# 528-column tiles for the high weight parts of a streamed decoder layer: five buffers at five offsets

## The chip, the cores and the metric

One core of a Trainium2 chip runs the whole kernel in one launch. The metric is the device time in microseconds (us) of one execution. The kernel before was timed three times: 2457.62, 2460.19 and 2460.8 us, median 2460.19 us. Addresses below are bytes within one SBUF partition.

## The reference

One decoder layer on 256 tokens of width 2048, in fp32. Cut to what matters, with D = 2048:

```
h  = rms_norm(x) * (1 + scale1) + shift1
z  = h @ w_in + b_in                       # combined input projection
y_attn = nsa_attention(q, k..., v...) @ w_nsa_out
y_conv = conformer_conv(a_glu) @ conv_pw_w + conv_pw_b
x  = x + gate1 * ((g0 * y_attn + g1 * y_conv) @ w_out)
h2 = rms_norm(x) * (1 + scale2) + shift2
# PEER: 16384 experts, 8 heads, 16 experts for each head and token
a    = einsum('td,ted->te', h2, u_emb[experts])
coef = gelu(a) * gate
out  = x + gate2 * einsum('te,ted->td', coef, v_emb[experts])
```

The kernel computes the PEER part densely: all 16384 rows of `u` and `v` are read, and a token's coefficient is zero for the experts that it did not choose.

## The kernel before

Nearly all of the work is TensorE (PE) matmuls whose weights stream in from HBM once. The class `Stream` (lines 129 to 219) walks a plan of weight pieces. A piece is 128 partitions x 512 columns of fp32. For each, SyncE loads half of a `raw` tile (line 149), ScalarE (ACT) rounds it to the type float32r as the high part `hi` (lines 152 and 153), and VectorE (DVE) computes the low part `lo` = raw - hi (lines 157 to 159). `hi` has five buffers, `lo` four, `raw` four of two pieces each. Three pieces are prepared ahead of the one that PE works on. There are 774 planned loads, so 1548 pieces. The order of everything is written out by hand: each call of `piece` issues the matmuls of one piece and then advances the side jobs (convolution, attention, top-k, and so on).

A piece is used in one of three ways:

- `proj` (lines 200 to 202), 524 pieces: `hi` and `lo` are the stationary operand, 128 columns at a time, and 256 token columns are the moving operand. Each piece gives 12 matmuls: hi x high activations, hi x low activations, lo x high activations, four times. In 32 of these pieces (the first eight half-head projections of `peer_wq`) the moving operand is `uhi` or `ulo`, 258 columns wide, so its start moves on by 1032 bytes from each k to the next.
- `proj2` (lines 213 and 217), 512 pieces of `u`: four matmuls with `hi` stationary and 512 moving columns of `h2`, then four with `lo` stationary and 256 moving columns.
- `products` (lines 1313 to 1315), 512 pieces of `v`: here `hi` and `lo` are the moving operand, 512 columns, and the coefficients `chi` and `clo` are stationary. For each of two token halves: chi x hi, chi x lo, clo x hi. For the first 49 rows of `v` (196 pieces) `chi` and `clo` lie in the pool `gg`, where they take the buffers that are called ohA, ohB, Ahi and Alo in the trace; for the other 79 rows (316 pieces) they lie in the pool `vp`.

Float32r matmuls read 4 bytes of the moving operand for each column and partition. A weight load (LDWEIGHTS) of 128 columns is part of every matmul and runs while the matmul before it streams.

Memory is handed out from both ends of the partition. `const` and `stream` lie at the low end, and the pools opened later with no side (`xp`, `adap`, `qkv`, `cp`, `attn`, `x1p`, `mp`, `tk`, `cb`) follow above them. The pools with `side="right"` come down from the high end. Sizes added up in that order give these starts, modulo 512 bytes:

| tiles | start modulo 512 before |
|---|---|
| `hi`, all five buffers (2048 bytes each) | 32 |
| `lo`, all four buffers | 32 |
| `hhi`, `hlo`, `ohi`, `olo`, `yhi`, `ylo`, `h2`: moving operands in pools from the right | 480 |
| `mhi`, `mlo`: moving operands of `w_out`, in `mp` (a pad tile of 448 bytes lies below them) | 480 |
| `uhi` for k = 0, 1, 2, ... | 160, 168, 176, ... |
| `chi`, `clo` in `gg` (v rows 0 to 48) | 480 |
| `chi`, `clo` in `vp` (v rows 49 to 127) | 288 |

Each 128-column slice of `hi` or `lo` is 512 bytes, so all slices of a buffer start at the same value.

Of the kernel before, what the change touches and what calls it, by code (L numbers as in the profile page):

```python
# [10 lines left out]
F32R = mybir.dt.float32r  # L11
# [61 lines left out]
def build(nc, tc, d):  # L73
# [19 lines left out]
    stream = P("stream")  # L93
# [33 lines left out]
    AHEAD = 3  # L127

    class Stream:
# [11 lines left out]
        def prefetch(self, to):  # L141

            last = 2 * len(self.chunks) - 1
            while self.hi_done <= min(to + 1, last):
                n = self.hi_done
                while self.loaded <= min(n // 2 + 3, len(self.chunks) - 1):
                    raw = stream.tile([128, 1024], F32, name="raw", tag="raw", bufs=4)
                    src, shape = self.chunks[self.loaded]
                    sp.dma_start(raw.rearrange("p (a b) -> p a b", a=shape[0]), src)
                    self.raw[self.loaded] = raw  # L150
                    self.loaded += 1
                hi = self.his[n] = stream.tile([128, 512], F32R, name="hi", tag="hi", bufs=AHEAD + 2)
                sc.copy(hi, self.source(n))  # L153
                self.hi_done += 1
            while self.lo_done <= min(to, last):
                n = self.lo_done
                lo = stream.tile([128, 512], F32R, name="lo", tag="lo", bufs=AHEAD + 1)
                hi = self.his.pop(n)
                ve.tensor_sub(lo, self.source(n), hi.bitcast(F32))  # L159
                self.parts[n] = (hi, lo)  # L160
                if n % 2:
                    del self.raw[n // 2]
                self.lo_done += 1
# [1271 lines left out]
```

## Time and profile before

| what | value |
|---|---|
| times of three runs | 2457.62, 2460.19, 2460.8 us |
| time of the profiled execution | 2459.97 us |
| its span, first to last instruction | 2458.2 us |
| PE busy | 2423.1 us (99%), 15324 matmuls |
| DVE busy | 1941.6 us (79%) |
| ACT busy | 1427.6 us (58%) |
| POOL busy | 140.4 us (6%) |
| HBM read | 533.41 MB, 219 GB/s over the span |

The profiled execution lies 1.8 us above its own span and 0.2 us below the median of the three runs. A matmul's duration in the profile runs from its start to the modelled end of its results, and matmuls overlap; the time that a matmul costs is the distance to the start of the next one, called its pitch here. In a stretch where PE is busy throughout, the mean pitch is the stretch plus one duration, divided by the number of matmuls that the view counts in it.

### The profile page before, as it was taken

How to read it: one execution, taken by the hardware profiler on the slowest of the kernel's cores; microseconds unless marked ns; L12 is line 12 of the kernel's file. 1: busy time of each engine (PE TensorE's matmuls, PEld its weight loads, DVE VectorE, ACT ScalarE, POOL GpSimd, SP SyncE). 2: the span in 40 equal slices, each digit the busy share in tenths (PEclk: the TensorE clock that was granted, in tenths of full speed). 3: DMA queues.
4: the chain of work that ended last, by engine and by line, in shares of the span. 5: the costliest groups of instructions: out<-in, count | busy, mean ns of one | idle time of the engine just before them, and what ended most of it. 6: DMA issues, size and time to landing. Idle time of an engine off the chain costs nothing.

```text
span 2458.2 us, 44220 instructions
## 1 busy us (share of the span) xinstructions
PE 2423.1 (99%) x15324; PEld 2152.0 (88%) x15324; DVE 1941.6 (79%) x4136; ACT 1427.6 (58%) x3198; POOL 140.4 (6%) x262
## 2 busy tenths in 40 slices
PE   6999999999999999999999999999999999999999
PEld 5899999888899999988888888888888888888887
DVE  7989897889788877899988888888655566666665
ACT  1045456667455566555568888887555555555554
POOL 0000000211222210000000000000000000100100
PEclk9999999999999999999999999999999999999999
DMA  9965556755888985555555555555555567777765
GB/s 374 400 222 192 186 190 196 242 176 188 300 298 306 322 275 170 186 190 187 192 189 173 178 173 180 174 179 173 189 193 191 192 211 243 241 243 242 243 204 195
DMA packets 155170, 540.49 MB, mean 220 GB/s; under 512 B 18753, under 2 KB 19009, under 8 KB 154689
## 3 DMA queue, kind: packets, MB, share of 16 engines
q1 hardware_dynamic: 134178, 467.40, 55.7%
q0 software_dynamic: 20768, 70.27, 9.1%
q8 instruction: 120, 1.97, 0.3%
q14 instruction: 104, 0.85, 0.1%
HBM read 533.41 MB, written 4.19 MB: 219 GB/s over the span
## 4 chain that ended last, share of the span: by engine, by line
PE 84%; issue 7%; DVE 5%; DMA 2%; POOL 2%; SPq 0%; POOLq 0%; ACT 0%; DVEq 0%
PE ps_acc L213 19%; PE ps_acc L217 10%; PE acc L200 7%; PE acc L202 7%; PE acc L201 7%; DVE acc L309 3%; PE ps_o L1315 2%; PE ps_s L1315 2%; PE ps_t L1315 2%; PE ps_o L1314 2%; PE ps_s L1314 2%; PE ps_t L1314 2%; PE ps_acc L1315 2%; PE ps_acc L1314 2%; PE ps_o L1313 2%
## 5 line engine op out<-in xcount | busy, mean ns | idle before, releaser
L153 ACT CAST hi<-raw 128x512 fp32r<-128x512 f32 x1548 | 956.1, 621 | 808.3 <-PE acc L201 246.5
L159 DVE TENSOR_TENSOR lo<-raw,hi 128x512 fp32r<-128x512 f32 x1548 | 1062.7, 688 | 390.6 <-PE ps_o L1314 78.4
L213 PE MATMUL ps_acc<-h,hi 128*128 128x512 f32 x2048 | 564.6, 397 | 0.0
L213 PEld LDWEIGHTS ps_acc<-h,hi 128*128 128x128 f32 x2048 | 346.7, 188 | 44.2
L217 PEld LDWEIGHTS ps_acc<-h,lo 128*128 128x128 f32 x2048 | 311.4, 188 | 46.4
L200 PE MATMUL acc<-hhi,hi 128*128 128x256 f32 x1200 | 345.7, 288 | 0.0
L202 PE MATMUL acc<-hhi,lo 128*128 128x256 f32 x1200 | 332.8, 277 | 0.2 <-DVE lo L159 0.2
L201 PE MATMUL acc<-hlo,hi 128*128 128x256 f32 x1200 | 332.8, 277 | 0.0
L217 PE MATMUL ps_acc<-h,lo 128*128 128x256 f32 x2048 | 318.0, 277 | 0.0
L200 PEld LDWEIGHTS acc<-hhi,hi 128*128 128x128 f32 x1200 | 225.7, 188 | 6.3 <-issue 5.3
L201 PEld LDWEIGHTS acc<-hlo,hi 128*128 128x128 f32 x1200 | 226.1, 188 | 3.2 <-issue 3.1
L202 PEld LDWEIGHTS acc<-hhi,lo 128*128 128x128 f32 x1200 | 225.4, 188 | 0.4 <-DVE lo L159 0.4
L371 POOL DMA_DIRECT2D adaw<-in_w_ada_dram x192 | 104.7, 546 | 774.3 <-DVE rr L719 277.3
L385 DVE SCALAR_TENSOR_TENSOR ada<-adaw,sc_c,ada 128x512 f32<-128x512 f32 x180 | 134.4, 746 | 14.4 <-DMA adaw<-in_w_ada_dram 13.9
L1290 POOL DMA_DIRECT2D g2w<-in_w_ada_dram x64 | 34.4, 538 | 1404.3 <-DVE Alo L123 1098.5
L1205 ACT ACTIVATE Ahi<-ohA,high 128x128 f16<-128x128 f16 x256 | 100.7, 393 | 10.4 <-PE ps_o L1226 10.2
L471 DVE SCALAR_TENSOR_TENSOR cacc<-glu,dwh,cacc 128x256 f32<-128x256 f32 x240 | 105.1, 475 | 0.0
L341 PE MATMUL zb<-hr,w 128*128 128x256 f32 x448 | 99.8, 381 | 0.0
L1205 ACT ACTIVATE Alo<-ohA,low 128x128 f16<-128x128 f16 x256 | 99.1, 387 | 0.0
L341 PEld LDWEIGHTS zb<-hr,w 128*128 128x128 f32 x448 | 84.5, 191 | 11.0
L309 DVE SCALAR_TENSOR_TENSOR acc<-wa,sc_c,acc 128x256 f32<-128x256 f32 x224 | 91.3, 478 | 0.0
L200 PE MATMUL acc<-ohi,hi 128*128 128x256 f32 x256 | 72.1, 282 | 3.7 <-DVE mr L903 3.7
(371 smaller groups left out, 4528.0 us busy)
## 6 DMA issues: line engine op xcount, KB each, us to landing
raw<-in_u_dram SPq DMA_DIRECT2D x256, 512.0 KB, 3.6
raw<-in_v_dram SPq DMA_DIRECT2D x256, 512.0 KB, 4.4
raw<-in_w_in_dram SPq DMA_DIRECT2D x150, 512.0 KB, 4.2
adaw<-in_w_ada_dram POOLq DMA_DIRECT2D x192, 256.0 KB, 5.0
wa<-in_w_ada_dram SPq DMA_DIRECT2D x64, 512.0 KB, 9.0
raw<-in_nsa_out_dram SPq DMA_DIRECT2D x32, 512.0 KB, 5.8
raw<-in_w_out_dram SPq DMA_DIRECT2D x32, 512.0 KB, 5.7
raw<-in_peer_wq_dram SPq DMA_DIRECT2D x32, 512.0 KB, 3.7
```

The lines of the kernel that those rows point to most:

```text
L153: sc.copy(hi, self.source(n))
L159: ve.tensor_sub(lo, self.source(n), hi.bitcast(F32))
L200: pe.matmul(ps, hi[:, o:o + 128], xhi[:, k], start=(k == 0), stop=False)
L201: pe.matmul(ps, hi[:, o:o + 128], xlo[:, k], start=False, stop=False)
L202: pe.matmul(ps, lo[:, o:o + 128], xhi[:, k], start=False, stop=(k == nk - 1))
L213: pe.matmul(ps.rearrange("p a t -> p (a t)"), hi[:, o:o + 128], x[:, k].rearrange("p a t -> p (a t)"), start=(k == 0), stop=False)
L217: pe.matmul(ps[:, 1], lo[:, o:o + 128], x[:, k, 0], start=False, stop=(k == nk - 1))
L309: ve.scalar_tensor_tensor(a, raw[:, i], c, a, op0=OP.mult, op1=OP.add)
L341: pe.matmul(zb[n // 2][:, n % 2], ws[k][n // 7][:, n % 7], hr[k], start=(k == 0 and n % 2 == 0), stop=(k == KT - 1), skip_group_check=True)
L1205: sc.activation(part[:, j], A[:, j], AF.Copy, scale=g[:, t0 + j:t0 + j + 1])
L1314: pe.matmul(ps, chi, lo, start=False, stop=False)
L1315: pe.matmul(ps, clo, hi, start=False, stop=(i1 == NK - 1))
```

## The change

The `hi` tile is allocated 528 columns wide, and its first 512 columns are used.

```
@@ -149,7 +149,7 @@
                     sp.dma_start(raw.rearrange("p (a b) -> p a b", a=shape[0]), src)
                     self.raw[self.loaded] = raw
                     self.loaded += 1
-                hi = self.his[n] = stream.tile([128, 512], F32R, name="hi", tag="hi", bufs=AHEAD + 2)
+                hi = self.his[n] = stream.tile([128, 528], F32R, name="hi", tag="hi", bufs=AHEAD + 2)[:, 0:512]
                 sc.copy(hi, self.source(n))
                 self.hi_done += 1
```

A buffer is then 2112 bytes, 64 more than four times 512. The five buffers start at 32, 96, 160, 224 and 288 modulo 512. All that lies above them at the low end moves up by 320 bytes: `lo` to 352, `mhi` and `mlo` to 288. The pools from the right stay where they are. The narrowest place, between the low and the high stack, is around the tiles `C1` and `C0`: 448 bytes before, 128 after. No instruction, wait, DMA or shape is added or removed.

## Rows read from the trace of the kernel before

**Rows 1.** The page, parts 1 and 2: busy us (share); PE and its clock in 40 slices.
```profile
PE 2423.1 (99%) x15324; PEld 2152.0 (88%) x15324; DVE 1941.6 (79%) x4136; ACT 1427.6 (58%) x3198; POOL 140.4 (6%) x262
PE   6999999999999999999999999999999999999999
PEclk9999999999999999999999999999999999999999
```
**Rows 2.** Groups of instructions by line: count, busy us, mean ns, idle before by releaser.
```profile
L159 DVE TENSOR_TENSOR lo<-raw,hi 128x512 fp32r<-128x512 f32 x1548 | 1062.7, 688 | 390.6 <-PE ps_o L1314 78.4 <-ACT hi L153 76.3 <-PE acc L202 58.9
L153 ACT CAST hi<-raw 128x512 fp32r<-128x512 f32 x1548 | 956.1, 621 | 808.3 <-PE acc L201 246.5 <-PE ps_acc L213 148.2 <-PE ps_o L1315 91.6
```
**Rows 3.** PE stretches: from:to us, length, busy (matmuls), clock, DMA share, GB/s.
```profile
160.00:208.00 48.00, 48.00 (x426) 1.00 0.58 193
1060.00:1240.00 180.00, 180.00 (x1041) 1.00 0.57 190
1800.00:2000.00 200.00, 200.00 (x876) 1.00 0.59 191
2060.00:2380.00 320.00, 320.00 (x1413) 1.00 0.72 238
```
**Rows 4.** Line 200 by tile: duration ns min/median/max, first to last start us, form.
```profile
L200 PE MATMUL acc<-hhi,hi x1200: 276/276/684, 148.7 to 803.7; 128*128 128x256 f32 x172
L200 PE MATMUL acc<-ohi,hi x256: 276/276/552, 642.8 to 814.5; 128*128 128x256 f32 x128
L200 PE MATMUL acc<-mhi,hi x256: 276/276/367, 814.9 to 905.7; 128*128 128x256 f32 x128
L200 PE MATMUL acc<-yhi,hi x128: 276/281/684, 560.1 to 631.0; 128*128 128x256 f32 x128
L200 PE MATMUL acc<-h,hi x128: 276/278/366, 956.3 to 1003.9; 128*128 128x256 f32 x128
```
**Rows 5.** Timeline of PE in a `proj` of `peer_wq`: start us, duration us, matmul.
```profile
962.72 0.28 PE L200 MATMUL acc<-h,hi 128*128 128x256 f32 x1
...
964.49 0.28 PE L200 MATMUL acc<-h,hi 128*128 128x256 f32 x1
```
**Rows 6.** Timeline of PE in a `proj` with 258 moving columns of `uhi` and `ulo`.
```profile
931.76 0.29 PE L200 MATMUL ps_o<-uhi,hi 128*128 128x258 f32 x1
...
933.92 0.28 PE L200 MATMUL ps_o<-uhi,hi 128*128 128x258 f32 x1
```
**Rows 7.** Line 213, the 512-column matmuls of `u`: duration ns min/median/max.
```profile
L213 PE MATMUL ps_acc<-h,hi x2048: 388/398/483, 1004.3 to 1748.9; 128*128 128x512 f32 x187
```
**Rows 8.** Timeline of PE where `chi` moves from `gg` (ohA) to `vp`.
```profile
2017.84 0.39 PE L1315 MATMUL ps_acc<-hi,ohB 128*128 128x512 f32 x1
...
2018.53 0.39 PE L1315 MATMUL ps_acc<-hi,ohB 128*128 128x512 f32 x1
2018.76 0.40 PE L1313 MATMUL ps_o<-hi,chi 128*128 128x512 f32 x1
2018.99 0.39 PE L1314 MATMUL ps_o<-lo,chi 128*128 128x512 f32 x1
...
2020.14 0.39 PE L1313 MATMUL ps_s<-hi,chi 128*128 128x512 f32 x1
```
**Rows 9.** Lines 153 and 159 alone: duration ns min/median/max, first to last start us.
```profile
L153 ACT CAST hi<-raw x1548: 601/622/701, 138.6 to 2445.7; 128x512 fp32r<-128x512 f32 x194
L159 DVE TENSOR_TENSOR lo<-raw,hi x1548: 627/691/696, 139.5 to 2446.9; 128x512 fp32r<-128x512 f32 x194
```

More of the change, by code (lines that the diff above doesn't have):

```diff
@@ L151, in prefetch @@
                     self.loaded += 1
-                hi = self.his[n] = stream.tile([128, 512], F32R, name="hi", tag="hi", bufs=AHEAD + 2)
+                hi = self.his[n] = stream.tile([128, 528], F32R, name="hi", tag="hi", bufs=AHEAD + 2)[:, 0:512]
                 sc.copy(hi, self.source(n))
```

## The prediction

> **What bounds the kernel now.** I read the page first: PE is busy for 2423.1 of 2458.2 us, at nine tenths or more in all slices but the first, and its clock shows nine in every slice [rows 1]. So the time is the sum of PE's pitches, and what the other engines do matters only where PE waits. Next the preparation: ACT's rounding and DVE's subtraction take 956.1 and 1062.7 us in all and wait mostly for PE to give a buffer back [rows 2]; they follow PE. Their durations hardly spread (median 622 of 601 to 701 ns, and 691 of 627 to 696 ns [rows 9]), so I see nothing in them that depends on which buffer they touch.
>
> Then the pitch, in stretches where PE never pauses. The granted clock is 1.00 there, the level of 2.4 GHz [rows 3]. Let the length plus one matmul's duration be divided by the count:
>
> - `proj`, 256 columns, 160 to 208 us: 48.28/426 = 113.3 ns. At 2.4 GHz this is 272 cycles, 17 for every 16 columns.
> - `u`, 1060 to 1240 us: 180.39/1041 = 173.3 ns, or 1.386 us for the eight matmuls of a piece. At the rate above, four of 512 and four of 256 columns would take 1.360 us. So 0.026 us of each `u` piece is excess.
> - `v` with coefficients in `gg`, 1800 to 2000 us: 200.39/876 = 228.8 ns. By the rate above 512 columns take 226.7 ns. Excess 2.1 ns a matmul, 0.013 us a piece.
> - `v` with coefficients in `vp`, 2060 to 2380 us: 320.39/1413 = 226.7 ns. No excess.
>
> The last two run the same instructions on the same `hi` and `lo`; what differs is that the stationary operand starts at 480 modulo 512 in one and at 288 in the other. The step between them lies in the open [rows 8]: three matmuls before it take 2018.53 - 2017.84 = 0.69 us, the six after it 2020.14 - 2018.76 = 1.38 us against 1.36 us at the rate, the first alone 0.23 us, and then the excess is gone for good. No wait shows there. I take from it that PE's pitch depends on where the stationary and the moving operand lie relative to each other, and that a new relation is settled into at a price.
>
> Two more stretches show the same. In `proj` of `peer_wq`, where all offsets are as elsewhere, 15 matmuls take 964.49 - 962.72 = 1.77 us, 118.0 ns each [rows 5], so one relation has two states, at 113.3 and at 118 ns. The duration shows which: its median is 276 ns for `hhi`, `ohi` and `mhi`, 281 for `yhi`, 278 for `h2` [rows 4]; most of `proj` is in the quick state. And where the moving operand starts 8 bytes further on at every k and its high and low parts differ, 18 matmuls of 258 columns take 933.92 - 931.76 = 2.16 us, 120.0 ns each [rows 6], against 258/256 x 113.3 = 114.2 ns at the rate: 5.8 ns of excess, with no settling.
>
> **The change, part by part.** Nothing is added to any queue. ACT writes and DVE reads the same 512 columns; I cost that at nothing, since 1548 of each show no spread by buffer [rows 9] and both have idle time [rows 2]. The buffers succeed each other as before, everything low moves by the same 320 bytes, and the two stacks still do not meet, so no wait changes its partner.
>
> What moves is the relation between `hi` and its partner. So far it is the same in every piece of a stage. After the change it differs from one piece to the next, five in turn, and within a piece `hi` and `lo` (352) differ as well. So every piece boundary is such a step as the one of [rows 8]. I price a step at that row's 0.02 us (1.38 - 1.36) and put it on all pieces but the 32 with `uhi`, which have no fixed relation to lose:
>
> - `proj`, (1200 + 256 + 256 + 128 + 128)/4 = 492 pieces [rows 4]: 492 x 0.02 = +9.8 us.
> - `u`, 512 pieces: they pay 0.026 us each already; I let the step replace this and count 0.
> - `v` in `gg`, 196 pieces: 0.02 - 0.013 = 0.007 each, +1.4 us.
> - `v` in `vp`, 316 pieces: +6.3 us.
>
> Sum +17.5 us. Against it, PE waits for `hi` or `lo` here and there in `proj` (maxima of 684 and 552 ns against medians of 276 [rows 4]) and in `u` (483 against 398 [rows 7]); a later PE finds its buffers ready, and some of the slow `proj` state goes. I take off 3.5 us for both, a fifth, as an estimate. The forecast is 2459.97 + 14 = 2474 us, as close to the median, 0.2 us away.
>
> Bounds of the price, since no row shows `hi` and `lo` at differing offsets: upward the 5.8 ns a matmul of the stretch that never settles [rows 6]; downward that excess vanishes wherever the offsets are far apart, as it does in `vp` [rows 3], so below nothing. My value lies nearest to [rows 8], because each piece keeps one relation for six to twelve matmuls, and that row shows six as enough to settle.
>
> The row says that a matmul is slowed by 10 to 20 ns in all when only an operand's address changes [rows 8]. The Trainium skill, "SBUF — State Buffer", section "Who interferes with whom", states that PE has two independent read ports, one for the moving operand and one for weight loads, and that PE never waits on anyone. By that rule the change would be worth nothing, and the sum would be 2460 us; the trace here speaks against it, and I keep it as a rival only.
>
> **Rivals.**
>
> - Nothing moves (2460 us). The excess would belong to the phase in which PE starts a stage, not to the addresses, and the step of [rows 8] would be chance. For: one relation has two states [rows 4, 5]. Against: the step falls on the very matmul where the address changes.
> - Faster (2446 us). The excess belongs to operands that lie within 64 bytes of each other modulo 512: 480 against 32 in `proj`, `u` and `v` in `gg`; in `vp`, 288 against 32, there is none [rows 3]. After the change four of five `hi` buffers and `lo` are further away in `proj` and `u`. `u` would give back four fifths of 512 x 0.026 = 13.3 us, 10.7 us; `proj` some 4 us of its slow state; `v` in `gg` 2 us; `v` in `vp`, now mixed (288 against 32 to 288 and 352), would lose 316 x 0.013 x 0.6 = 2.5 us. Sum -14 us. It decides if a step between two distant relations costs under some 0.009 us, so that 1516 of them stay below 14 us. Against: the `uhi` stretch has its operands 128 bytes and more apart and is the slowest of all [rows 6].
> - Much slower (2513 us). No piece settles: 5.8 ns on each of 5904 `proj` matmuls (34 us) and 1896 in `vp` (11 us), 5.8 - 2.1 on 1176 in `gg` (4 us), 5.8 - 3.3 on 4096 in `u` (10 us), less the same absorbed part, some 6 us: +53 us. Against: every relation that lasts has settled so far.
>
> The change could also fail to do what it says if the allocator rounded the tile up to 2560 bytes; then nothing would move, and the first rival's time holds.
>
> **How the numbers follow.** Forecast (a price for each step, +5 to +35 us) 0.45; nothing 0.19; faster 0.25; much slower 0.11. Slower holds the first and the last, 0.56. Differences below 0.2% (4.9 us) can't be told from no change. The forecast's own range is 2465 to 2495 us. For 8 in 10, I leave out the lower half of the faster case and most of the much slower one: 2444 to 2500 us.
>
> **What the profile after would show.** Right: the stretch of `v` in `vp` rises from 226.7 to some 230 ns a matmul; `proj` durations of 281 ns and above become common where 276 ruled; `u` stays near 1.386 us a piece; ACT and DVE durations stay. Wrong: `u` near 1.36 us a piece (the faster rival), or all four stretches as now (nothing). If `proj` pitches come out near 119 ns throughout, no piece settles. I would also be wrong if PE began to wait for `hi` longer than now.

## The result, and the profile after

The changed kernel takes 2499.36 us (median of four runs, 2498.34 to 2500.42) against 2460.49 us before: a ratio of 1.0157, 95% interval 1.0143 to 1.017. It is 39 us slower where 14 were forecast. The profiled execution took 2498.34 us, its span is 2496.6 us, 38.4 more than before. The order of the instructions on each engine and the bytes read from HBM are as before.

The page of the changed kernel, parts 1 and 2, against [rows 1]:

```profile
PE 2467.4 (99%) x15324; PEld 2184.6 (88%) x15324; DVE 1947.7 (78%) x4136; ACT 1428.1 (57%) x3198; POOL 140.3 (6%) x262
...
PE   7999999999999999999999999999999999999999
...
PEclk8999999999999999999999999999999999999999
```

As many matmuls as before, at the same clock in all slices but the first (8 where 9 stood). PE is busy for 44.3 us longer and its weight loads for 32.6, DVE for 6.1, ACT and POOL for less than 1 us. The two groups of the preparation, against [rows 2]:

```profile
L153 ACT CAST hi<-raw 128x512 fp32r<-128x512 f32 x1548 | 954.9, 620 | 851.0 <-PE acc L201 274.4
L159 DVE TENSOR_TENSOR lo<-raw,hi 128x512 fp32r<-128x512 f32 x1548 | 1064.9, 689 | 426.4 <-ACT hi L153 82.0
```

620 and 689 ns where 621 and 688 stood: ACT and DVE do not care where the buffers lie. They only wait longer, ACT for PE and DVE for PE and ACT. So the loss is in PE's pitch. The stretches of busy PE, against [rows 3] (columns as there, the second and the last begin 20 and 30 us later, as their stages do):

```profile
160.00:208.00 48.00, 48.00 (x408) 1.00 0.57 186
1080.00:1260.00 180.00, 180.00 (x1026) 1.00 0.58 187
1800.00:2000.00 200.00, 200.00 (x865) 1.00 0.58 189
2090.00:2400.00 310.00, 310.00 (x1337) 1.00 0.72 234
```

With one duration added, as before: `proj` 48.28/408 = 118.3 ns (113.3 before), `u` 180.39/1026 = 175.8 ns or 1.407 us a piece (1.386), `v` in `gg` 200.40/865 = 231.7 ns (228.8), `v` in `vp` 310.40/1337 = 232.2 ns (226.7). All four stages lose. The lines by tile, against [rows 4] and [rows 7] (duration min/median/max in ns, first to last start in us):

```profile
L200 PE MATMUL acc<-hhi,hi x1200: 277/282/684, 147.2 to 814.9; 128*128 128x256 f32 x172
L200 PE MATMUL acc<-mhi,hi x256: 276/281/367, 826.6 to 921.0; 128*128 128x256 f32 x128
L200 PE MATMUL ps_o<-uhi,hi x64: 277/283/367, 921.3 to 958.8; 128*128 128x258 f32 x64
L213 PE MATMUL ps_acc<-h,hi x2048: 387/393/482, 1020.6 to 1773.7; 128*128 128x512 f32 x187
L1313 PE MATMUL ps_o<-hi,chi x158: 388/396/401, 2047.0 to 2453.1; 128*128 128x512 f32 x158
L1313 PE MATMUL ps_o<-hi,ohA x50: 388/397/398, 1774.4 to 2042.1; 128*128 128x512 f32 x50
```

Before, the lines that [rows 4] and [rows 7] do not have were:

```profile
L200 PE MATMUL ps_o<-uhi,hi x64: 277/284/366, 906.0 to 943.5; 128*128 128x258 f32 x64
L1313 PE MATMUL ps_o<-hi,chi x158: 389/389/398, 2018.8 to 2415.4; 128*128 128x512 f32 x158
L1313 PE MATMUL ps_o<-hi,ohA x50: 388/388/397, 1749.6 to 2014.0; 128*128 128x512 f32 x50
```

The median of `hhi` went from 276 to 282 ns, that of `ps_o` in `v` from 388 and 389 to 397 and 396. First starts mark the stages: `proj` up to the first `mhi` now lasts 826.6 - 147.2 = 679.4 us, 13.2 more than before; `w_out` (from the first `mhi` to the first `uhi`) 94.7 us, +3.5; `u` 1774.4 - 1020.6 = 753.8 us, +8.5; `v` in `gg` 2047.0 - 1774.4 = 272.6, +3.4; `v` in `vp` 2496.6 - 2047.0 = 449.6, +10.1. `peer_wq` adds 1.0, and PE's first `hhi` comes 1.5 us sooner. In what follows these lengths (the last one up to the end of the span) are the measure; in two kernels whose stage has the same offsets modulo 256 they agree to 0.1 us in `u` and in `v` in `vp`, to 1.1 in `gg`, and to some 3 us in `proj`, where PE waits at times and where one relation has two states [rows 5].

### The profile page after: what moved, and what is told of

It reads as the page before. It is cut to its first block, busy times and chain, and to the rows that moved or that the text cites. A ratio compares the mean times of both kernels' runs of the same rounds, so it can differ in the third digit from the quotient of the medians.

```text
span 2496.6 us, 44220 instructions
## 1 busy us (share of the span) xinstructions
PE 2467.4 (99%) x15324; PEld 2184.6 (88%) x15324; DVE 1947.7 (78%) x4136; ACT 1428.1 (57%) x3198; POOL 140.3 (6%) x262
## 4 chain that ended last, share of the span: by engine, by line
PE 92%; DVE 6%; DMA 1%; issue 1%; ACT 0%; SPq 0%; DVEq 0%
PE ps_acc L213 19%; PE ps_acc L217 10%; PE acc L200 9%; PE acc L201 9%; PE acc L202 9%; DVE acc L309 3%; PE ps_s L1313 2%; PE ps_t L1313 2%; PE ps_o L1313 2%; PE ps_o L1315 2%; PE ps_s L1315 2%; PE ps_t L1315 2%; PE ps_acc L1313 2%; PE ps_acc L1315 2%; PE ps_t L1314 2%; PE ps_s L1314 2%
## 5 line engine op out<-in xcount | busy, mean ns | idle before, releaser
L153 ACT CAST hi<-raw 128x512 fp32r<-128x512 f32 x1548 | 954.9, 620 | 851.0 <-PE acc L201 274.4
L217 PE MATMUL ps_acc<-h,lo 128*128 128x256 f32 x2048 | 328.4, 282 | 0.0
L309 DVE SCALAR_TENSOR_TENSOR acc<-wa,sc_c,acc 128x256 f32<-128x256 f32 x224 | 91.4, 479 | 0.0
```

Source lines behind the costliest of these rows:

```text
L217: pe.matmul(ps[:, 1], lo[:, o:o + 128], x[:, k, 0], start=False, stop=(k == nk - 1))
L309: ve.scalar_tensor_tensor(a, raw[:, i], c, a, op0=OP.mult, op1=OP.add)
```

## The experiments

Only addresses differ in the kernels below, unless the text says more. R is the start of the stationary operand less that of the moving one, modulo 256. Before, R is 64 in `proj` and `u` (32 - 480), 192 in `v` in `gg` (480 - 32) and 0 in `v` in `vp` (288 - 32).

**The parts of the change.** One kernel moves `lo` to 352, and `mhi` and `mlo` above it to 288, with `hi` as before.

```
                 hi = self.his[n] = stream.tile([128, 512], F32R, name="hi", tag="hi", bufs=AHEAD + 2)
+                if n == 0:
+                    stream.tile([128, 80], F32, name="pad")
```

> hi keeps 512 columns and its one offset (32); a pad of 320 bytes behind hi moves lo and all above it as the change does (lo 352, mhi and mlo 288). A, a price for each piece whose relation differs from the last: every piece is like the one before, so it settles, about 2460 us, proj at 113 to 115 ns a matmul. B, a price for each matmul whenever successive matmuls have operands at differing offsets: hi and lo differ in every piece, so most of the loss of the change stands, about 2490 us, proj near 118 ns. C, a price that belongs to the value of the relation: the matmuls of u that load lo stay at 120 ns as in the changed kernel, those that load hi go back, about 2475 us.

2498.91 us, ratio 1.0158 (1.0142 to 1.0175): as much as the whole change, with all `hi` buffers at one offset.

The other spreads `hi` alone; `lo`, `mhi` and `mlo` keep their offsets.

```
+    hip = P("hip")
...
-                hi = self.his[n] = stream.tile([128, 512], F32R, name="hi", tag="hi", bufs=AHEAD + 2)
+                hi = self.his[n] = hip.tile([128, 528], F32R, name="hi", tag="hi", bufs=AHEAD + 2)[:, 0:512]
...
-    mp.tile([128, 112], F32, name="head")
+    mp.tile([128, 32], F32, name="head")
```

> The five offsets of hi alone: hi lies in a pool of its own above lo, so lo stays at 32, and a smaller pad leaves mhi and mlo at 480. A: as the changed kernel, 2495 to 2500 us, since hi still changes from piece to piece. B: hi and lo differ in four pieces of five instead of five, about 2490 us. C: the 256-column matmuls of u, which load lo at 32 against 480, go back from 120 to 115 ns, about 10 us less than the changed kernel, 2488 us; proj between 114 and 118 ns.

2491.32 us, ratio 1.0129 (1.0113 to 1.0146). The two parts cost 40 and 32 us alone and 39 together; they do not add. By stage (`proj`, `u`, `v` in `gg`, `v` in `vp`) the first kernel takes 681.6, 751.8, 271.8 and 449.2 us, the second 677.7, 748.7, 271.8 and 448.3; before, it was 666.2, 745.3, 269.2 and 439.5.

**The same value in every piece.** Two kernels shift `hi` and `lo` together, so that no relation changes at a piece boundary or within a piece.

```
     stream = P("stream")
+    stream.tile([128, 80], F32, name="pad")
```

> One pad of 320 bytes below raw: hi and lo both at 352, all buffers alike, mhi and mlo at 288. Every matmul of a stage has one and the same relation. A and B: it settles, about 2460 us, proj near 113 to 115 ns. C: the relation 352 against 480 costs 120 ns for each 256-column matmul in proj and u, about 2500 us.

> One pad of 192 bytes below raw: hi and lo both at 224, 256 bytes from the moving operands at 480 in proj and u and from the weights at 480 in v's first rows; 64 bytes from the weights at 288 in v's other rows. A and B: about 2460 us, within 10 us, whichever state each stage settles into. C: the distance of 256 that has no excess in v gives none in u either, 13 us less there, v's other rows lose 0.013 us a piece, 4 us: about 2450 us.

The first (`hi` and `lo` at 352, 80 columns) takes 2494.98 us, ratio 1.014 (1.0123 to 1.0157); the second (at 224, 48 columns) 2497.7 us, ratio 1.0153 (1.0137 to 1.017). Without a single step between relations the loss is there. Stretches of busy PE with 352:

```profile
160.00:208.00 48.00, 48.00 (x407) 1.00 0.58 186
1080.00:1260.00 180.00, 180.00 (x1028) 1.00 0.58 188
1800.00:2000.00 200.00, 200.00 (x859) 1.00 0.58 188
2090.00:2400.00 310.00, 310.00 (x1356) 1.00 0.74 238
```

and with 224:

```profile
160.00:208.00 48.00, 48.00 (x403) 1.00 0.58 181
1080.00:1260.00 180.00, 180.00 (x1030) 1.00 0.59 188
1800.00:2000.00 200.00, 200.00 (x884) 1.00 0.61 193
2090.00:2400.00 310.00, 310.00 (x1330) 1.00 0.72 233
```

With 224, `proj` has 48.28/403 = 119.8 ns. The two parts of `v`, the same instructions, have changed places: 200.39/884 = 226.7 ns in `gg`, where the excess used to be, and 310.40/1330 = 233.4 ns in `vp`, where there was none. Line 1313 of that kernel (1314 there) by tile shows the same in the durations, 389 against 397 ns in the median:

```profile
L1314 PE MATMUL ps_o<-hi,chi x158: 388/397/398, 2044.0 to 2452.1; 128*128 128x512 f32 x158
L1314 PE MATMUL ps_o<-hi,ohA x50: 389/389/396, 1777.4 to 2039.3; 128*128 128x512 f32 x50
```

So the theory of the prediction, a price for each change of relation, could not stand as the main cause. The new one: each value of the relation has its own pitch, paid by every matmul. To test it, five kernels with other widths of the same pad, and one that leaves `hi` and `lo` alone and moves the other side down by 192 bytes:

```
+    rpad = P("rpad", side="right")
+    rpad.tile([128, 48], F32, name="pad")
     hp = P("hp", side="right")
```

> One pad of 64 bytes below raw: hi and lo at 96, all buffers alike; mhi and mlo move along (32). With R = stationary start minus moving start, modulo 512: proj and u have 128, v with weights in gg 384, v with weights in vp 192, w_out 64 as before. Theory V, the price belongs to R alone: w_out stays near 114.4 ns; v in gg, proj and u show what 384, 128 and 192 cost; v in vp is not above 235 ns; total 2480 to 2505 us. Theory F, the layout before is a lucky phase that any edit disturbs: all stages, w_out too, near 118 ns and 232 ns.

> One pad of 128 bytes below raw: hi and lo at 160. R is 192 in proj and u, 320 in v with weights in gg, 128 in v with weights in vp, 64 in w_out. V: v in vp has the R of 128 that cost 233.3 ns in v with weights in gg where hi and lo lay at 352, so 233 ns here; w_out near 114.4; total 2485 to 2505 us. F: w_out near 118 ns, v near 232 ns in both parts.

> One pad of 256 bytes below raw: hi and lo at 288. R is 320 in proj and u, 192 in v with weights in gg, 0 in v with weights in vp, 64 in w_out. V: w_out near 114.4 ns; v in gg the same pitch as v in vp of the run with a pad of 64 bytes, since both have 192; proj between 117 and 121 ns; total 2485 to 2510 us. F: w_out near 118 ns.

> hi and lo as before; a pad of 192 bytes at the top of the stack from the right moves the other side instead: hhi, hlo, ohi, olo, yhi, ylo, h2 and the coefficients in gg from 480 to 288, the coefficients in vp from 288 to 96. R is 256 in proj and u, as in the run with hi and lo at 224, 256 in v with weights in gg, 64 in v with weights in vp, 64 in w_out (nothing moves there). V: stage by stage the times of that run within 2 us, total about 2497 us: 119.8 ns in proj, 226.7 ns in v in gg, 233.3 ns in v in vp. If the absolute place of hi and lo counts: near 2460 us.

> One pad of 32 bytes below raw: hi and lo at 64, between the four places tried so far. R modulo 256 is 96 in proj and u, 160 in v with weights in gg, 224 in v with weights in vp, 64 in w_out. If the pitch follows R smoothly, proj lies between its values at 64 and 128, 115 to 118 ns, u near 749 us, v in vp between 439 and 443 us: about 2475 us. If what counts is 64-byte steps only, proj is as at 64 or as at 128, 114.5 or 118.9 ns. If a start on a multiple of 64 bytes helped PE in itself, v, whose moving operand then has one, drops below 226 ns.

> One pad of 224 bytes below raw: hi and lo at 256. R modulo 256 is 32 in proj and u, 224 in v with weights in gg, 32 in v with weights in vp, 64 in w_out. Smooth: proj between its values at 0 and 64, 115 to 119 ns, v in vp between 439 and 452 us, about 2475 to 2490 us. Steps of 64: proj as at 0 or at 64, 119.8 or 114.5 ns.

The starts of `hi` and `lo` modulo 512 are in the second column; the last four columns are lengths of stages in us, each with its R in brackets. "One run" stands beside a before of 2462.06 (first four of them) or 2461.8 us.

| kernel | `hi`, `lo` | time, us | `proj` | `u` | `v` in `gg` | `v` in `vp` |
|---|---|---|---|---|---|---|
| before | 32 | 2460.49 | 666.2 (64) | 745.3 (64) | 269.2 (192) | 439.5 (0) |
| pad 64 columns | 288 | 2463.21, one run | 669.5 (64) | 745.3 (64) | 269.2 (192) | 439.4 (0) |
| pad 16 | 96 | 2494.33, one run | 684.4 (128) | 752.7 (128) | 273.3 (128) | 443.5 (192) |
| pad 80 | 352 | 2494.98 | 683.9 (128) | 752.7 (128) | 274.4 (128) | 443.5 (192) |
| pad 32 | 160 | 2489.47, one run | 679.7 (192) | 745.4 (192) | 274.4 (64) | 450.0 (128) |
| pad 48 | 224 | 2497.7 | 686.9 (0) | 751.3 (0) | 266.6 (0) | 451.7 (64) |
| other side moved by 192 | 32 | 2499.95, one run | 688.6 (0) | 751.3 (0) | 266.6 (0) | 451.7 (64) |
| pad 8 | 64 | 2506.63, one run | 682.4 (96) | 756.3 (96) | 274.4 (160) | 451.8 (224) |
| pad 56 | 256 | 2500.99, one run | 680.7 (32) | 753.0 (32) | 274.4 (224) | 451.7 (32) |

Three things are to be read here. A shift by 256 bytes changes nothing in `u` and `v` (for this kernel 2485 to 2510 us were expected, by a period of 512). Wherever R is the same, `u` and `v` in `vp` have the same length to 0.1 us, whether the relation was made by 16 or 80 columns of pad, or from the other side: it is the distance that counts. The two parts of `v` confirm it: against R = 0, a piece costs 0.040 us more in `gg` and 0.039 us more in `vp` with 64, and 0.013 us in both with 192. And the cheap values depend on the stage: 64 and 192 in `u`, 64 in `proj`, 0 in both parts of `v`; 0 is the dearest in `proj`. Of the eight placements, those of before and 256 bytes away from it are the cheap ones. Between steps of 64 bytes the price does not run smoothly: with 32 and with 96, `u` takes 753.0 and 756.3 us, more than with 0, 64 or 128.

In `proj` the link is looser. With 64 columns of pad R is 64 as before, and yet the stretch from 160 to 208 us has 410 matmuls, 117.8 ns each: this relation has the slower pitch of [rows 5] too, and only the whole stage (666.2 and 669.5 us, against 679.7 to 688.6 for the other values) sets it apart.

Two rivals can be read off the same traces. Had the layout before been a lucky phase that any edit disturbs, `w_out` would be slower in all these kernels. There R stays at 64, since `mhi` and `mlo` move along with `hi` and `lo` or stay with them, and it takes 91.4 to 93.1 us, against 91.1 before and 94.7 after the change. And had PE been slowed by ACT and DVE writing the next `hi` and `lo` at the same offsets, the pitch would be shorter while they rest. In the kernel with 352, 172 matmuls of `hhi` and `hlo` in `proj` ran while no instruction of ACT, DVE or POOL did: 118.9 ns each, against 118.8 where ACT or DVE was preparing pieces throughout (distances with a pause left out). In `v` in `vp` with 224 it is 232.5 against 232.6 ns.

**A difference of 256 within a piece, and the other part of `v`.** With 64 columns between `hi` and `lo`, `lo` starts at 288 and `hi` at 32: apart modulo 512, alike modulo 256.

```
                 hi = self.his[n] = stream.tile([128, 512], F32R, name="hi", tag="hi", bufs=AHEAD + 2)
+                if n == 0:
+                    stream.tile([128, 64], F32, name="pad")
```

> hi stays at 32; a pad of 256 bytes behind hi puts lo at 288, mhi and mlo at 224. Modulo 512 hi and lo differ by more than in any buffer of the change but one; modulo 256 they agree, and every relation of before is kept. Period 256: within 5 us of before, 2460 us, stage by stage the same pitches. Period 512, or a price for differing offsets as such: proj at 117 to 119 ns, about 2490 us.

2460.57 us (median of ten runs) against 2461.8, ratio 0.9992 (0.9983 to 1.0001): no difference, against the 40 us of 80 columns in the same place.

If R = 0 is the cheap value of `v`, the part in `gg` can be given it, by two pads that move `chi` and `clo` there from 480 to 288. `h2` and the coefficients in `vp` move by 256 bytes with them, so their R stays:

```
     gg = P("gg", side="right")
+    gg.tile([128, 16], F32, name="pad0")
...
                 parts = [gg.tile(SH, F16, name=n, tag=n, bufs=1) for n in ("Ahi", "Alo")]
+                if t0 == 0:
+                    gg.tile([128, 48], F32, name="pad1")
```

> hi and lo as before; two pads in gg (192 bytes above, 64 below) put the coefficients of v's first 49 rows at 288 instead of 480, so R modulo 256 becomes 0 there, as it is in v's other rows, and move h2 and all below by 256 bytes, which keeps R there. The price by R: v in gg falls from 269.2 to 266.6 us, all else stays: 2.6 us less than before, ratio 0.9989. A lucky phase: any other result, most likely slower.

2458.51 us (median of eleven runs) against 2461.8, ratio 0.9987 (0.9978 to 0.9996). `v` in `gg` takes 266.6 us instead of 269.2, the other stages are as before. Its stretches of `v`:

```profile
1800.00:2000.00 200.00, 200.00 (x884) 1.00 0.60 194
2090.00:2400.00 310.00, 310.00 (x1370) 1.00 0.73 233
```

884 matmuls in 200 us where 876 were [rows 3], 226.7 ns, and the rate itself in both parts. It is the fastest kernel of this study, 0.13% below before.

Third, 32 columns in the place between `hi` and `lo`: `lo` at 160, R = 192, where `hi` has 64; in `u` both values are cheap alone.

> hi stays at 32 (R = 64 modulo 256 in proj and u); a pad of 128 bytes behind hi puts lo at 160 (R = 192 there), mhi and mlo at 96. Both R alone cost the same in u, 745.3 and 745.4 us, and 114.5 and 117.8 ns in proj. V, the price is the mean of the values: u near 745 us, proj (without w_out) near 115.6 ns, total about 2468 us. M, operands that alternate between two R cost more than either: u above 748 us, proj at 118 ns or more, total about 2490 us.

2474.39 us, ratio 1.0061 (1.0044 to 1.0078). `proj` 663.0 us, `u` 748.7, `v` in `gg` 271.0, `v` in `vp` 451.6. `u` is 3.4 us longer than with either value alone, and `v` in `vp` longer than the mean of its values (two thirds at 439.5, one at 450.0: 443.0) by 8.6. `proj` is shorter than with either value. So mixing values in a piece has an effect of its own, most plainly in `vp`, which is longer than with either value alone.

**The piece boundary alone.** Four kernels ask whether a boundary costs something by itself. In three of them `hi` and `lo` of a piece share a start, which is 32 in even pieces and 160, 96 or 288 in odd ones; so the relation changes at every boundary and nowhere else. For this, `hi` has four buffers, and its rounding comes one piece later. The fourth kernel is the control, with only that.

```
-            while self.hi_done <= min(to + 1, last):
+            while self.hi_done <= min(to, last):
...
+                if n == 1:
+                    stream.tile([128, 32], F32, name="pad")
+                hi = self.his[n] = stream.tile([128, 512], F32R, name="hi", tag="hi%d" % (n % 2), bufs=2)
...
+                if n < 2:
+                    stream.tile([128, 96 if n == 0 else 32], F32, name="pad%d" % n)
+                lo = stream.tile([128, 512], F32R, name="lo", tag="lo%d" % (n % 2), bufs=2)
...
+    mp.tile([128, 80], F32, name="head")
```

(160 in odd pieces; for 96 the widths are 16, 112, 16 and 96, for 288 they are 64, 64, 64 and 48.)

> Control for the three runs beside it: hi has four buffers and is rounded one piece later, all starts as before modulo 512. Expected: the stages as before, proj up to mhi 666 us, u 745 us, v in gg 269 us, v in vp 439.5 us, in all 2460 us. If PE came to wait for hi, the stages would be longer by that, and the three runs are read against this one.

> hi and lo of a piece share a start; it is 32 in even pieces and 160 in odd ones, so the relation changes at every piece boundary and nowhere else. If only the values count, each stage is the mean of the lengths measured with one value throughout: proj up to mhi 673 us (666 and 680), u 745 us (745.3 at both values), v in gg 271.8 us (269.2 and 274.4), v in vp 444.8 us (439.5 and 450.0), in all some 2475 us. If each boundary costs the 0.02 us of the prediction, on top of that: u 755.6, gg 275.7, vp 451.1, proj 10 us more, in all some 2505 us.

> As the run with 160, with 96 in odd pieces, as two neighbouring buffers of the change lie. Values alone: proj up to mhi 675 us, u 749.0 us (745.3 and 752.7), v in gg 271.5 us, v in vp 441.5 us (439.5 and 443.5), in all some 2477 us. With 0.02 us for each boundary: u 759, gg 275.4, vp 447.8, in all some 2507 us.

> As the run with 160, with 288 in odd pieces: at every boundary the start changes by 256 modulo 512 and stays the same modulo 256. Values modulo 256 alone: every stage as in the control, 2460 us. If any change of the relation modulo 512 were a step of 0.02 us: u 755.5, gg 273.1, vp 445.8, proj 676, in all some 2490 us.

One run each, beside a before of 2460.9 us. In brackets stands what the values alone would give: the mean of the two lengths in the table above, plus what the control is longer than before in that stage.

| odd pieces | time, us | `proj` | `u` | `v` in `gg` | `v` in `vp` |
|---|---|---|---|---|---|
| control | 2467.66 | 671.9 | 745.3 | 269.3 | 440.1 |
| 288 | 2471.93 | 675.6 (671.9) | 745.3 (745.3) | 269.3 (269.3) | 440.1 (440.1) |
| 160 | 2481.55 | 672.1 (678.7) | 749.9 (745.4) | 271.3 (271.9) | 447.3 (445.4) |
| 96 | 2494.53 | 677.2 (680.9) | 752.0 (749.0) | 272.5 (271.7) | 448.2 (442.1) |

The control's 7 us lie in `proj` and `w_out`, where `hi` is now late at times. Stretches of busy PE with 288 in odd pieces:

```profile
1080.00:1260.00 180.00, 180.00 (x1040) 1.00 0.59 190
1800.00:2000.00 200.00, 200.00 (x875) 1.00 0.60 192
2090.00:2400.00 310.00, 310.00 (x1369) 1.00 0.72 236
```

and with 160:

```profile
1080.00:1260.00 180.00, 180.00 (x1031) 1.00 0.58 188
1800.00:2000.00 200.00, 200.00 (x869) 1.00 0.58 190
2090.00:2400.00 310.00, 310.00 (x1347) 1.00 0.71 233
```

A boundary across which the start moves by 256 costs nothing in `u` and `v`. (The 3.7 us in `proj` are not settled: its stretch from 160 to 208 us has 410 matmuls, 117.8 ns each, the slower pitch of [rows 5], which one relation can have.) A boundary across which R changes costs 4.5/512 = 0.009 and 3.0/512 = 0.006 us in `u`, 1.9/316 = 0.006 and 6.1/316 = 0.019 us in `v` in `vp`, about nothing in `gg`, and below nothing in `proj`. So in `u` and `vp` the boundaries do cost something, and the values cost too. In `proj` the values do not add up like this: with 160 in odd pieces the mean pitch is 114.5 ns, as in the control (114.6), though 192 alone gives 117.8.

## Why the prediction was right and wrong

**What held.** The bound: PE is the bound in both kernels, ACT and DVE keep their durations, and the loss is PE's pitch alone. The cause lies in the relation of the two operands' starts. The signs that the prediction named appeared in part: `v` in `vp` rose (to 232 ns, not 230), the median of `hhi` went to 282 ns. But `u` did not stay near 1.386 us a piece (1.407), and `proj` at 118.3 ns came near the 119 that was named as the sign of a piece that never settles. That the direction came out right is partly luck: the prediction had no idea that the layout before was among the cheap ones. That 2499 us lies just inside its widest range, 2444 to 2500, is owed to the much slower rival, which it held for unlikely.

**The step that failed** is the one from [rows 8] to the price: "So every piece boundary is such a step", at 0.02 us, with each relation free once it has settled. Those rows show R going from 192 to 0 in `v`. They were the passage from a dear value to the free one, and what was read as a stage's own excess (2.1 ns in `gg`) was the price of its value: with R = 0 it is gone. [rows 3] had the sign already: in `gg` one relation lasts for 196 pieces and keeps its excess to the end. A relation that lasts does not become free, as the kernels with one value throughout show. The layout before happened to have the cheap value in `proj`, `u` and `v` in `vp`; I took these for what any lasting relation gives. Every other layout tried was dear, but the one 256 bytes away, and the change puts one `hi` buffer at each of three other values, and all of `lo` at one.

**The terms.** The values of the change, from the table: `hi` has R = 64, 128, 192, 0, 64 in `proj` and `u`, 192, 128, 64, 0, 192 in `v` in `gg`, 0, 192, 128, 64, 0 in `vp`; `lo` has 128, 128 and 192. Weighting `hi` with two thirds of the time (2 of 3 matmuls, or 4 of 512 columns against 4 of 256) and `lo` with one:

| stage | forecast | mean of the values | measured |
|---|---|---|---|
| `proj` up to `mhi` | part of +9.8 | 679.3, +13.1 | 679.4, +13.2 |
| `w_out`, `peer_wq` | part of +9.8 | not measured by value | +3.5, +1.0 |
| `u` | 0 | 749.6, +4.3 | 753.8, +8.5 |
| `v` in `gg` | +1.4 | 271.7, +2.5 | 272.6, +3.4 |
| `v` in `vp` | +6.3 | 444.4, +4.9 | 449.6, +10.1 |

By this mean the values make up some 25 us of the 38, and `w_out` and `peer_wq` another 4.5. The 10 us beyond it are 0.008 us a piece in `u`, 0.005 in `gg` and 0.016 in `vp`, as large as the boundaries of the last four kernels, and nothing in `proj`. So the forecast's price was of the right size where it was read, in `v` in `vp`, and twice too large or more in `u`.

The division is an estimate, and other kernels show how loose it is. With only `lo` moved, every piece is like the one before it, and still the stages lie 9.4, 4.0, 1.1 and 8.4 us beyond the same mean: there the values explain 11 of the 34 us that these stages lose, and what is left cannot come from pieces that differ from each other. With only `hi` spread it is 4.4, 1.6, 1.6 and 5.3 us. In `proj` the mean misses by 9.4 us one way there and by 7.7 the other way with `lo` at 160, so that its agreement for the change may be chance. In `u` two thirds to one is not the right weight: with 128 throughout, the 256-column matmuls of `lo` go from 114.7 to 118.1 ns and the 512-column ones of `hi` only from 232.3 to 232.6 (116.1 and 230.9 with 192, 118.4 and 231.7 with 0). With a price for each kind of matmul, `u` would be 752.3 us with only `lo` moved (751.8 measured), 748.2 with `lo` at 160 (748.7) and 751.6 after the change (753.8). How the loss divides between the values and their mixing is thus not shown. That both play a part is shown in `vp`: one value throughout costs up to 12.2 us there, and with only `lo` moved the stage is longer than with either of its two values alone (439.5 and 443.5).

`u` was counted at 0, because its excess of 0.026 us a piece was taken for a step already paid. It was another thing: with R = 64 its 512-column matmuls have a mean pitch of 232.3 ns and its 256-column ones 114.7 ns; after the change 231.4 and 119.9 ns (means over the trace, distances with a pause left out). The long ones gained 0.9 ns each and the short ones lost 5.2.

The part taken off, 3.5 us, was about right: the mean pitch of `proj` grew from 114.5 to 118.3 ns (in `w_out` from 113.5 to 118.2; means over the trace, distances with a pause left out), which on 5136 and 768 matmuls is 23 us, and the stages grew by 17.7; some 5 us went into shorter waits.

**The rivals.** That nothing moves is out. There I named the Trainium skill, "SBUF — State Buffer", section "Who interferes with whom", where PE's two read ports are independent and PE waits on nobody. The runs speak against the independence as a rule for times: with the same instructions at a granted clock of 1.00, `v` in `vp` runs at 226.7 or at 233.4 ns a matmul according to the distance of the two operands. What in the memory or in PE makes that so, no run here shows. That PE waits on nobody agrees with the equal pitch, 118.9 and 118.8 ns, with ACT and DVE at rest and at work. The faster rival had the wrong rule (nearness modulo 512): with `hi` and `lo` at 288, no distance at all from the coefficients in `vp`, that stage takes 439.4 us as before, without excess, and with 256 between the operands `proj` is at its slowest. The much slower one had the right idea, a price on every matmul, and 5.8 ns was near the size: 5.0 ns in the stretch of `proj`, 5.5 in `vp`, 2.9 in `gg`, but 2.5 in `u`. It took it for a piece that never settles, and made it 34 us in `proj` where the mean pitch, part of which was slow before, grew by some 4 ns: 23 us, less the shorter waits. The tile of 2112 bytes is what the change says; were it 2560 bytes, the stages would not have moved.

**What stays open.** Why the period is 256, why the cheap values differ between stages, why mixing values costs in `vp`, and why in `proj` it costs in one kernel and gains in another. Starts of `hi` and `lo` that are no multiple of 32 were not tried, and no run sets apart the DMA writes into `raw`.

## What to carry to other kernels

Where PE runs without a pause, compare its pitch stage by stage with the quickest stage of the same shape, and look at the distance between the stationary and the moving operand modulo 256 bytes: here a shift by 32 bytes cost 45 us of 2460, and two pads gave 3. A pad of any width in a pool moves everything above it, so after a change to one tile's size, list the starts of all matmul operands before and after. And a stage that is free of excess does not show that every layout would be: give a stage another layout before a rule is made of one transition.

## What was not expected of the hardware

- The pitch of a float32r matmul depends on the distance between its operands' starts modulo 256 bytes: 512 columns in `v` take 226.7 to 233.4 ns in steady stretches, 256 columns in `proj` 113.3 to 119.8 ns, at the same clock and with both operands in SBUF. In `proj` one distance (64) was seen at 113.3 and at 118 ns.
- A matmul's modelled duration goes up with the dear values (276 and 283 ns, 389 and 397 ns in the medians), so that these can be seen in the view by line without a timeline. A small excess does not show: in `gg` before, at 228.8 ns, the median is 388.
- A change of the relation between pieces cost 0.006 to 0.019 us in `u` and `vp` if it changed the value modulo 256, and nothing if it did not (one run of each kernel).
